# A squared-ReLU MLP on one Trainium2 core: accumulators, unit order and priorities around its first product

## The chip, the core and the metric

The kernel runs on one core of a Trainium2 chip. The metric is the device time of one execution in microseconds (us). In the traces PE is TensorE (matmuls), DVE is VectorE, ACT is ScalarE, POOL is GpSimd and SP issues the DMAs. Each of these engines works through its own list of instructions in order; an instruction that waits holds up all that stand behind it on that engine.

## The reference

One decoder block over 512 tokens of width 1024: two attention mixers, then an MLP of inner width 4096, all in float32.

```python
h = modulate(rmsnorm(x, g_mix), sh_a, sc_a); z = h @ w_in
...  # NSA and MLA attention, gated sum y
x = x + gt_a * (y @ w_out)
h = modulate(rmsnorm(x, g_mlp), sh_m, sc_m)
x = x + gt_m * (square(relu(h @ w_fc1)) @ w_fc2)
return rmsnorm(x, g_final)
```

The change concerns the line with `w_fc1` and `w_fc2` alone.

## The kernel before

**Arithmetic.** Values lie feature by feature on the 128 partitions with the 512 tokens along the row. A float32 operand is split into a rounded part (`hi`, written by ACT) and a rest (`lo`, written by DVE), and each product is three matmuls: hi by hi, hi by lo, lo by hi (`mm3`, L196 to L199). The split of a weight tile starts from its raw load (`w_raw`, four buffers) and stands in `wsplit` (L183 on ACT, L184 on DVE).

**Stages of the MLP.** The inner width is worked off in four quarters (`qq`, L953), which I call q0 to q3. A quarter has eight units of 128 inner features. A unit is a product of 24 matmuls with 512 columns into one accumulator in PSUM (`dense`, lines L197 to L199); in q0 the first four units are computed together in four accumulators. Then `unit_parts` (L908) turns the accumulator into operands of the second product: relu (L911, ACT), squares, differences, and hi and lo parts. Units 0 to 3 give `uh`, `ul` (L923, L924); unit k+4 gives its own `uh`, `ul` (L932, L933) and, together with the stored parts of unit k, the operands called t2, t3 and t4 (L940 to L948).

**Second product.** It takes two output features blocks at a time (`fc2_pair`), by a scheme of seven products instead of eight (Winograd's form of Strassen's algorithm), each of 12 matmuls with 256 columns (L854). Its weights need four sums of raw weight blocks (`wsum`, L825, POOL), each split into `ws_hi` (L811, ACT) and `ws_lo` (L812, DVE). A quarter has four such pairs; q3 has two, and its other four output blocks are done at the end by plain products (L977 on). The seven products accumulate in four half tiles: pa and pb (tag `s`), pc and pd (tag `t`). In the first pair of a quarter (`fresh`) they are interleaved, with a loop that takes the first three of the four inner blocks ahead of the last one (L868). The sums `u` and `e` in `ue` are built outside: copies on ACT (L864, L867), additions on DVE (L873: `e += pc`, L874: `u += pd`), then `v` and the outputs `xr` (L893 to L900). The addition of L873 has to read pc before the last product (a22 by t4) goes on accumulating there.

**What sets the order.** A scheduler lays out each engine's list when the program is built; instructions under `tc.high_priority()` go ahead of others that are ready. Tiles are handed out by tag from a fixed number of buffers: in PSUM two for `acc`, two for `s`, two for `t`, one each for `o` and `m`. The raw weights share four buffers, freed when both splits and the sums have read them.

Of the kernel before, what the change touches and what calls it, by code (L numbers as in the profile page):

```python
# [12 lines left out]
AF = mybir.ActivationFunctionType  # L13
ALU = mybir.AluOpType
PSUM = bass.MemoryType.PSUM

P = 128
S = 512
D = 1024
KT = D // P  # L20
# [18 lines left out]
NPRE = 4  # L39
FAR = 2  # L40
# [6 lines left out]
def block_kernel(ctx: ExitStack, tc: tile.TileContext, d):  # L47
    nc = tc.nc
# [3 lines left out]
    def psum(tag):  # L52
        bufs = PB[tag]
        return ps.tile([P, S], F32, name="ps_" + tag, tag=tag, bufs=bufs)
# [237 lines left out]
    for j in range(4):  # L292
        t = big_n(f"qn{j}")
# [401 lines left out]
    for step in ORDER.split():  # L695
        op, a = step[0], int(step[1:] or 0)
# [35 lines left out]
    for i in range(8):  # L732
        if i < 4:
            t = sb.tile([P, 1280], F32R, name="ohl", tag="p", bufs=NB["p"])[:, 0:1024].rearrange("p (a b) -> p a b", a=2)
# [67 lines left out]
            nc.scalar.activation(xt[n][:, tok], xt[n][:, tok], AF.Copy, scale=cols[:, C_GFIN + n:C_GFIN + n + 1])  # L802

    HS = S // 2
    T0, T1 = HALVES
    ngt = sb.tile([P, KT], F32, name="ngt")
    nc.vector.tensor_scalar(ngt, modb[:, GTM:GTM + KT], -1.0, None, op0=ALU.mult)
# [6 lines left out]
    def pair_weights(src0, src1):  # L814

        raw = [wtile() for _ in range(2)]
        nc.sync.dma_start(raw[1], src1)
        nc.sync.dma_start(raw[0], src0)
        a11, a12 = raw[0][:, 0:S], raw[0][:, S:D]
        a21, a22 = raw[1][:, 0:S], raw[1][:, S:D]  # L820
        sums = []
        for x_, y_ in ((a21, a22), (a11, a21), (0, a11), (2, a12)):
            t = sb.tile([P, S], F32, name="wsum", tag="pT", bufs=NB["pT"])
            with tc.high_priority():
                nc.gpsimd.tensor_tensor(t, sums[x_] if isinstance(x_, int) else x_, y_, op=ALU.add)  # L825
            sums.append(t)
        out = {}

        def part(hi, lo):
            pat = dict(a=4, b=P)  # L830
            return hi.rearrange("p (a b) -> p a b", **pat), lo.rearrange("p (a b) -> p a b", **pat)

        hi = sb.tile([P, D], F32R, name="w_hi", tag="w_hi", bufs=NB["hi"])
        lo = sb.tile([P, D], F32R, name="w_lo", tag="w_lo", bufs=NB["lo"])
        split_part(raw[0], hi, lo)
        out["a11"] = part(hi[:, 0:S], lo[:, 0:S])
        out["a12"] = part(hi[:, S:D], lo[:, S:D])
        for names, ids in ((("s1", "s3"), (0, 1)), (("s2", "s4"), (2, 3))):
            hi = sb.tile([P, 1280], F32R, name="ws_hi", tag="p", bufs=NB["p"])
            lo = sb.tile([P, 1280], F32R, name="ws_lo", tag="p", bufs=NB["p"])  # L840
            for j, (nm_, i) in enumerate(zip(names, ids)):
                c = slice(S * j, S * j + S)
                split_part(sums[i], hi[:, c], lo[:, c])
                out[nm_] = part(hi[:, c], lo[:, c])
        hi = sb.tile([P, D], F32R, name="w_hi", tag="w_hi", bufs=NB["hi"])
        lo = sb.tile([P, D], F32R, name="w_lo", tag="w_lo", bufs=NB["lo"])
        split_part(a22, hi[:, 0:S], lo[:, 0:S])
        out["a22"] = part(hi[:, 0:S], lo[:, 0:S])
        return out

    def product(out, w, x, first, ks=range(4)):
        for k in ks:
            for j, (a_, b_) in enumerate(((0, 0), (0, 1), (1, 0))):
                nc.tensor.matmul(out, w[a_][:, k], x[k][b_], start=(first and k == 0 and j == 0),  # L854
                                 stop=(k == 3 and j == 2), skip_group_check=True)

    def pair_tiles(w, b, sink, fresh):

        pa, pb = psum("s")[:, 0:HS], psum("s")[:, 0:HS]
        pc, pd = psum("t")[:, 0:HS], psum("t")[:, 0:HS]  # L860
        ue = tmp("ue")
        u, e = ue[:, 0:HS], ue[:, HS:S]
        product(pa, w["a11"], b["11"], True)
        nc.scalar.activation(u, pa, AF.Copy)  # L864
        product(pb, w["s1"], b["t1"], True)
        if fresh:
            nc.scalar.activation(e, pb, AF.Copy)  # L867
            for ks in (range(3), range(3, 4)):  # L868
                product(pa, w["a12"], b["21"], False, ks)
                product(pb, w["s4"], b["22"], False, ks)  # L870
                product(pc, w["s3"], b["t3"], True, ks)
                product(pd, w["s2"], b["t2"], True, ks)
            nc.vector.tensor_tensor(e, e, pc, op=ALU.add)  # L873
            nc.vector.tensor_tensor(u, u, pd, op=ALU.add)  # L874
        else:
            product(pc, w["s3"], b["t3"], True)
            nc.scalar.activation(e, pc, AF.Copy)
            nc.vector.tensor_tensor(e, e, pb, op=ALU.add)
            product(pd, w["s2"], b["t2"], True)
            nc.vector.tensor_tensor(u, u, pd, op=ALU.add)  # L880
            product(pa, w["a12"], b["21"], False)
            product(pb, w["s4"], b["22"], False)
        product(pc, w["a22"], b["t4"], False)
        sink(pa, pb, pc, u, e)
# [23 lines left out]
    def unit_parts(n, pa, ub, keep, last):  # L908

        r = tmp("relu")  # L910
        nc.scalar.activation(r, pa, AF.Relu)  # L911
        hh = big_n(f"uh{n}", F32R)
        hl = big_n(f"ul{n}", F32R)
        if n < 4:
            if n < 3:
                raw = small_c(f"ur{n}")
            else:
                raw = sb.tile([P, S], F32, name="ur3", tag="qst", bufs=NB["qst"])
            b12 = keep["b12"][:, n * HS:n * HS + HS]
            nc.scalar.activation(b12, r[:, T1], AF.Square)  # L920
            nc.scalar.activation(raw[:, T0], r[:, T0], AF.Square)
            nc.vector.tensor_tensor(raw[:, T1], raw[:, T0], b12, op=ALU.subtract)
            nc.scalar.activation(hh, raw, AF.Copy)  # L923
            nc.vector.tensor_tensor(hl, raw, f(hh), op=ALU.subtract)  # L924
            ub["11"].append((hh[:, T0], hl[:, T0]))
            ub["t1"].append((hh[:, T1], hl[:, T1]))
            keep["raw"].append(raw)
            keep["b12s"].append(b12)
            return
        k = n - 4  # L930
        nc.scalar.activation(r, r, AF.Square)
        nc.scalar.activation(hh, r, AF.Copy)  # L932
        nc.vector.tensor_tensor(hl, r, f(hh), op=ALU.subtract)  # L933
        ub["21"].append((hh[:, T0], hl[:, T0]))
        ub["22"].append((hh[:, T1], hl[:, T1]))

        raw, b12 = keep["raw"][k], keep["b12s"][k]
        t2, t4 = raw[:, T1], raw[:, T0]
        t3 = tmp("t3")[:, T0] if last else b12
        nc.vector.tensor_tensor(t3, r[:, T1], b12, op=ALU.subtract)  # L940
        nc.vector.scalar_tensor_tensor(t2, t2, -1.0, r[:, T1], op0=ALU.mult, op1=ALU.subtract)
        nc.vector.scalar_tensor_tensor(t4, t2, -1.0, r[:, T0], op0=ALU.mult, op1=ALU.subtract)
        t3p = big_n(f"t3{k}", F32R)
        nc.scalar.activation(t3p[:, T0], t3, AF.Copy)
        nc.vector.tensor_tensor(t3p[:, T1], t3, f(t3p[:, T0]), op=ALU.subtract)
        th_ = sb.tile([P, 2, S], F32R, name="t24", tag="kk", bufs=4)
        nc.scalar.activation(th_[:, 0], raw, AF.Copy)
        nc.vector.tensor_tensor(th_[:, 1], raw, f(th_[:, 0]), op=ALU.subtract)  # L948
        ub["t2"].append((th_[:, 0, T1], th_[:, 1, T1]))
        ub["t4"].append((th_[:, 0, T0], th_[:, 1, T0]))  # L950
        ub["t3"].append((t3p[:, T0], t3p[:, T1]))

    for qq in range(4):  # L953
        ub = {c: [] for c in ("11", "21", "22", "t1", "t2", "t3", "t4")}
        keep = dict(b12=sb.tile([P, D], F32, name="b12", tag="cb"), raw=[], b12s=[])
        pre = {}
        if qq == 0:
            ws = [wsplit(d["w_fc1"][n], (KT, P), n < FAR) for n in range(NPRE)]
            pre = {n: psum(("acc", "acc", "s", "s")[n]) for n in range(NPRE)}
            for tok in HALVES:  # L960
                for k in range(KT):
                    for n in range(NPRE):
                        mm3(pre[n][:, tok], (ws[n][0][:, k], ws[n][1][:, k]),
                            (h2[k][0][:, tok], h2[k][1][:, tok]), k == 0, k == KT - 1)
        for n in range(8):
            if n in pre:
                pa = pre[n]
            else:
                w = wsplit(d["w_fc1"][8 * qq + n], (KT, P))
                pa = psum("acc")  # L970
                dense(pa, w, h2)
            unit_parts(n, pa, ub, keep, qq == 3)
        nf = KT - NH2 if qq == 3 else KT
        for n in range(0, nf, 2):
            fc2_pair(qq, n)
# [138 lines left out]
```

## Time and profile before

| what | value |
|---|---|
| median of 3 runs | 853.53 us (853.52 to 855.48) |
| the profiled execution's own time | 856.97 us |
| its span from first to last instruction | 855.2 us |
| PE busy | 806.6 us, 94% |
| DVE busy | 614.0 us, 72% |
| ACT busy | 394.7 us, 46% |
| POOL busy | 137.6 us, 16% |
| mean granted TensorE clock | 0.981 |

The span leaves out 1.8 us around the program, and the profiled execution is 3.4 us above the median. Times inside the trace are counted from the start of the span. [...] The MLP runs from about 480 us to the end.

### The profile page before, as it was taken

How to read it: one execution, taken by the hardware profiler on the slowest of the kernel's cores; microseconds unless marked ns; L12 is line 12 of the kernel's file. 1: busy time of each engine (PE TensorE's matmuls, PEld its weight loads, DVE VectorE, ACT ScalarE, POOL GpSimd, SP SyncE). 2: the span in 40 equal slices, each digit the busy share in tenths (PEclk: the TensorE clock that was granted, in tenths of full speed). 3: DMA queues.
4: the chain of work that ended last, by engine and by line, in shares of the span. 5: the costliest groups of instructions: out<-in, count | busy, mean ns of one | idle time of the engine just before them, and what ended most of it. 6: DMA issues, size and time to landing. Idle time of an engine off the chain costs nothing.

```text
span 855.2 us, 11874 instructions
## 1 busy us (share of the span) xinstructions
PE 806.6 (94%) x4444; PEld 649.1 (76%) x4444; DVE 614.0 (72%) x1193; ACT 394.7 (46%) x742; POOL 137.6 (16%) x109
## 2 busy tenths in 40 slices
PE   6899999999999999999799989999989998999896
PEld 3687668665586657888679978897789878987795
DVE  6979569878658873568875858866777487757864
ACT  4458436556226443222323556435733464346651
POOL 2400000000001000003300030613242143404100
PEclk8999999999999999999989998999999999999998
DMA  9773342000141204687564121333223322322302
GB/s 337 259 247 111 126 146 73 27 25 30 45 134 64 79 33 160 205 272 217 171 223 152 66 75 50 99 123 99 74 75 122 101 74 74 124 99 77 96 1 99
DMA packets 31003, 99.75 MB, mean 117 GB/s; under 512 B 3521, under 2 KB 5761, under 8 KB 30946
## 3 DMA queue, kind: packets, MB, share of 16 engines
q1 hardware_dynamic: 30880, 98.89, 35.0%
q8 instruction: 35, 0.57, 0.3%
q0 software_dynamic: 64, 0.11, 0.1%
q14 instruction: 22, 0.18, 0.1%
q10 hardware_dynamic: 2, 0.00, 0.0%
HBM read 96.89 MB, written 2.10 MB: 116 GB/s over the span
## 4 chain that ended last, share of the span: by engine, by line
PE 67%; DVE 14%; ACT 6%; POOL 5%; DMA 4%; issue 3%; SPq 0%; POOLq 0%; DVEq 0%; ACTq 0%
PE ps_acc L197 11%; PE ps_acc L198 10%; PE ps_acc L199 10%; PE ps_s L854 7%; PE ps_t L854 6%; POOL wsum L825 4%; PE ps_t L391 3%; PE ps_o L568 3%; DVE junk L107 3%; DVE ws_lo L812 3%; PE ps_s L640 2%; PE ps_o L653 2%; DMA w_raw<-in_w_ada_dram 2%; DMA w_raw<-in_w_fc_dram 2%; POOL yb L758 1%
## 5 line engine op out<-in xcount | busy, mean ns | idle before, releaser
L183 ACT ACTIVATE w_hi<-w_raw 128x1024 fp32r<-128x1024 f32 x76 | 80.2, 1058 | 134.7 <-PE ps_acc L198 96.2
L184 DVE TENSOR_TENSOR w_lo<-w_raw,w_hi 128x1024 fp32r<-128x1024 f32 x76 | 96.7, 1275 | 63.6 <-ACT w_hi L183 63.6
L197 PE MATMUL ps_acc<-h2h,w_hi 128*128 128x512 f32 x224 | 88.9, 397 | 7.7 <-ACT relu L911 7.7
L198 PE MATMUL ps_acc<-h2l,w_hi 128*128 128x512 f32 x224 | 88.4, 395 | 0.0
L199 PE MATMUL ps_acc<-h2h,w_lo 128*128 128x512 f32 x224 | 88.2, 394 | 0.0
L346 ACT ACTIVATE p<-p,nm 128x128 f32<-128x128 f32 (+3 forms) x96 | 53.3, 556 | 58.2 <-DVE nm L344 56.9
L198 PE MATMUL ps_acc<-hl,w_hi 128*128 128x512 f32 x200 | 80.1, 400 | 0.0
L199 PE MATMUL ps_acc<-hh,w_lo 128*128 128x512 f32 x200 | 80.0, 400 | 0.0
L197 PE MATMUL ps_acc<-hh,w_hi 128*128 128x512 f32 x200 | 79.4, 397 | 0.0
L825 POOL TENSOR_TENSOR wsum<-w_raw 128x512 f32<-128x512 f32 x28 | 40.4, 1447 | 176.1 <-DMA w_raw<-in_w_fc_dram 148.7
L379 DVE COPY pT<-ps_t 128x512 f32<-128x512 f32 (+1 forms) x72 | 42.4, 598 | 31.3 <-PE ps_o L568 16.6
L811 ACT ACTIVATE ws_hi<-wsum 128x512 fp32r<-128x512 f32 x56 | 35.4, 631 | 63.8 <-POOL wsum L825 57.5
L825 POOL TENSOR_TENSOR wsum<-wsum,w_raw 128x512 f32<-128x512 f32 x28 | 48.4, 1727 | 85.4 <-DVE ws_lo L812 85.1
L812 DVE TENSOR_TENSOR ws_lo<-wsum,ws_hi 128x512 fp32r<-128x512 f32 x56 | 55.0, 1011 | 7.5 <-PE ps_acc L198 6.3
L197 PEld LDWEIGHTS ps_acc<-h2h,w_hi 128*128 128x128 f32 x224 | 42.7, 191 | 18.2 <-ACT relu L911 9.4
L107 DVE SCALAR_TENSOR_TENSOR junk<-w_raw,cb 128x1024 bf16<-128x1024 f32 x32 | 40.0, 1255 | 15.3 <-DMA w_raw<-in_w_ada_dram 15.1
L199 PEld LDWEIGHTS ps_acc<-h2h,w_lo 128*128 128x128 f32 x224 | 42.8, 191 | 9.1
L198 PEld LDWEIGHTS ps_acc<-h2l,w_hi 128*128 128x128 f32 x224 | 42.8, 191 | 8.7
L198 PEld LDWEIGHTS ps_acc<-hl,w_hi 128*128 128x128 f32 x200 | 37.6, 188 | 10.9 <-issue 4.3
L199 PEld LDWEIGHTS ps_acc<-hh,w_lo 128*128 128x128 f32 x200 | 37.6, 188 | 10.0 <-issue 3.1
L197 PEld LDWEIGHTS ps_acc<-hh,w_hi 128*128 128x128 f32 x200 | 37.6, 188 | 9.9 <-issue 3.0
L854 PE MATMUL ps_t<-t,ws_hi 128*128 128x256 f32 x224 | 41.1, 281 | 0.0
(457 smaller groups left out, 2108.7 us busy)
## 6 DMA issues: line engine op xcount, KB each, us to landing
w_raw<-in_w_fc_dram SPq DMA_DIRECT2D x64, 512.0 KB, 3.3
w_raw<-in_w_ada_dram SPq DMA_DIRECT2D x32, 512.0 KB, 4.2
w_raw<-in_w_z_dram SPq DMA_DIRECT2D x25, 512.0 KB, 3.8
w_ada<-in_w_ada_dram SPq DMA_DIRECT2D x16, 512.0 KB, 6.1
w_raw<-in_w_c_dram SPq DMA_DIRECT2D x8, 512.0 KB, 4.4
w_raw<-in_w_o_dram SPq DMA_DIRECT2D x8, 512.0 KB, 4.2
w_raw<-in_w_out_dram SPq DMA_DIRECT2D x8, 512.0 KB, 3.5
w_raw<-in_w_g_dram SPq DMA_DIRECT2D x8, 448.0 KB, 6.7
```

What stands on the lines that cost most here:

```text
L107: nc.vector.scalar_tensor_tensor(junk, w, 1.0, cb, op0=ALU.mult, op1=ALU.mult, accum_out=mod[:, col:col + 1])
L183: nc.scalar.activation(hi[:, :n], raw[:, :n], AF.Copy)
L184: nc.vector.tensor_tensor(lo[:, :n], raw[:, :n], f(hi[:, :n]), op=ALU.subtract)
L197: nc.tensor.matmul(out, w[0], x[0], start=first, stop=False)
L198: nc.tensor.matmul(out, w[0], x[1], start=False, stop=False)
L199: nc.tensor.matmul(out, w[1], x[0], start=False, stop=last)
L346: nc.scalar.activation(o, o, AF.Exp, bias=nm, scale=-1.0, accum_out=sm)
L379: nc.vector.tensor_copy(dst, src)
L811: nc.scalar.activation(hi, src, AF.Copy)
L812: nc.vector.tensor_tensor(lo, src, f(hi), op=ALU.subtract)
L825: nc.gpsimd.tensor_tensor(t, sums[x_] if isinstance(x_, int) else x_, y_, op=ALU.add)
L854: nc.tensor.matmul(out, w[a_][:, k], x[k][b_], start=(first and k == 0 and j == 0), stop=(k == 3 and j == 2), skip_group_check=True)
```

## The change

It has five parts. The units of a quarter are computed in the order 0 4 1 5 2 6 3 7 (and their weights loaded so). The accumulators of the units rotate over four places, two of tag `acc` and the single buffers of `m` and `o`. The relu gets high priority and the weight sums on POOL lose it. The subtraction that begins t3 goes from DVE to POOL. In the first pair of a quarter pc comes before pb in the loop, pd's whole product follows after the loop, and `e += pc` gets high priority.

```diff
+    UNITS = (0, 4, 1, 5, 2, 6, 3, 7)
@@ pair_weights
-            with tc.high_priority():
-                nc.gpsimd.tensor_tensor(t, sums[x_] if isinstance(x_, int) else x_, y_, op=ALU.add)
+            nc.gpsimd.tensor_tensor(t, sums[x_] if isinstance(x_, int) else x_, y_, op=ALU.add)
@@ pair_tiles, if fresh
             for ks in (range(3), range(3, 4)):
                 product(pa, w["a12"], b["21"], False, ks)
+                product(pc, w["s3"], b["t3"], True, ks)
                 product(pb, w["s4"], b["22"], False, ks)
-                product(pc, w["s3"], b["t3"], True, ks)
-                product(pd, w["s2"], b["t2"], True, ks)
-            nc.vector.tensor_tensor(e, e, pc, op=ALU.add)
+            with tc.high_priority():
+                nc.vector.tensor_tensor(e, e, pc, op=ALU.add)
+            product(pd, w["s2"], b["t2"], True)
             nc.vector.tensor_tensor(u, u, pd, op=ALU.add)
@@ unit_parts
-        nc.scalar.activation(r, pa, AF.Relu)
+        with tc.high_priority():
+            nc.scalar.activation(r, pa, AF.Relu)
...
-        nc.vector.tensor_tensor(t3, r[:, T1], b12, op=ALU.subtract)
+        nc.gpsimd.tensor_tensor(t3, r[:, T1], b12, op=ALU.subtract)
@@ the loop over quarters
-            ws = [wsplit(d["w_fc1"][n], (KT, P), n < FAR) for n in range(NPRE)]
+            ws = [wsplit(d["w_fc1"][UNITS[n]], (KT, P), n < FAR) for n in range(NPRE)]
...
-        for n in range(8):
-            if n in pre:
-                pa = pre[n]
+        for i, n in enumerate(UNITS):
+            if i in pre:
+                pa = pre[i]
             else:
                 w = wsplit(d["w_fc1"][8 * qq + n], (KT, P))
-                pa = psum("acc")
+                pa = psum(("acc", "acc", "m", "o")[i % 4])
                 dense(pa, w, h2)
             unit_parts(n, pa, ub, keep, qq == 3)
```

The lines of the changed kernel stand one or two below those of the kernel before (the relu is L913, `e += pc` still L873, `u += pd` L875).

**First place: ACT in q1, from the weights of the last unit but some on.** Before, the list around the relu of the fourth unit (numbers behind a name tell buffers apart, `b` is the tile b12):

```order
L183 ACTIVATE w_hi<-w_raw 128x1024
L811 ACTIVATE ws_hi<-wsum 128x512 x3
L911 ACTIVATE relu<-ps_acc 128x512
L920 ACTIVATE b_5119<-relu 128x256
L921 ACTIVATE ur_5278<-relu 128x256
L923 ACTIVATE uh_5276<-ur_5278 128x512
L183 ACTIVATE w_hi<-w_raw 128x1024
```

Now, from the relu of the fourth unit in time (unit 5) to the operand of the seventh (unit 3, `uh_5417`):

```order
L913 ACTIVATE relu<-ps_o 128x512
L812 ACTIVATE ws_hi<-wsum 128x512 x3
L933 ACTIVATE relu<-relu 128x512
...
L183 ACTIVATE w_hi<-w_raw 128x1024
L913 ACTIVATE relu<-ps_acc 128x512
...
L913 ACTIVATE relu<-ps_acc 128x512
L812 ACTIVATE ws_hi<-wsum 128x512
L933 ACTIVATE relu<-relu 128x512
L934 ACTIVATE uh_5370<-relu 128x512
...
L925 ACTIVATE uh_5417<-ur_5419 128x512
```

The relu now stands ahead of the splits of the weight sums, and the work behind the relu (squares, `uh`) behind them. The weights of the eighth unit (the last `w_hi` of the first list, the only L183 of the second) stood behind the short parts of unit 3, three operations, and stand behind the parts of unit 5 now: its square, its `uh`, t3 and t24. Unit 3, which was fourth, is seventh, and its `uh` comes behind a `ws_hi` of the second pair and the parts of unit 6.

**Second place: DVE in the first pair of q1.** Before:

```order
L893 SCALAR_TENSOR_TENSOR xr_3166<-ps_s,modb,xr_3166 128x256
L812 TENSOR_TENSOR w_lo<-w_raw,w_hi 128x512
L812 TENSOR_TENSOR ws_lo<-wsum,ws_hi 128x512 x3
L873 TENSOR_TENSOR ue<-ue,ps_t 128x256
L812 TENSOR_TENSOR ws_lo<-wsum,ws_hi 128x512
L874 TENSOR_TENSOR ue<-ue,ps_t 128x256
L897 TENSOR_TENSOR v_5600<-ue,ps_s 128x256
```

Now:

```order
L894 SCALAR_TENSOR_TENSOR xr_3166<-ps_s,modb,xr_3166 128x256
L873 TENSOR_TENSOR ue<-ue,ps_t 128x256
L813 TENSOR_TENSOR ws_lo<-wsum,ws_hi 128x512 x2
L813 TENSOR_TENSOR w_lo<-w_raw,w_hi 128x512
L813 TENSOR_TENSOR ws_lo<-wsum,ws_hi 128x512 x2
L875 TENSOR_TENSOR ue<-ue,ps_t 128x256
L900 TENSOR_TENSOR v_5598<-ue,ps_t 128x256
L813 TENSOR_TENSOR w_lo<-w_raw,w_hi 128x1024
L898 TENSOR_TENSOR v_5600<-ue,ps_s 128x256
```

`e += pc` (L873) moved ahead of all five splits of weights; `u += pd` (L874, now L875) stands behind all five instead of four, and the `v` that frees pb (L897, now L898) behind six, one of them of 1024 columns.

**Third place: POOL in q2.** Now, with the subtraction L942 between the sums:

```order
L942 TENSOR_TENSOR b_6004<-relu,b_6004 128x256
L825 TENSOR_TENSOR wsum<-w_raw 128x512 x2
L825 TENSOR_TENSOR wsum<-wsum,w_raw 128x512 x2
L942 TENSOR_TENSOR b_6004<-relu,b_6004 128x256
L825 TENSOR_TENSOR wsum<-w_raw 128x512 x2
L825 TENSOR_TENSOR wsum<-wsum,w_raw 128x512
L942 TENSOR_TENSOR b_6004<-relu,b_6004 128x256 x2
```

Before, POOL had no L942; the second one now stands behind the four sums of a pair's weights, the last two behind three more.

## Rows read from the trace of the kernel before

**Rows 1.** The page's line on the engines: busy us, share of the span, instructions.

```profile
PE 806.6 (94%) x4444; PEld 649.1 (76%) x4444; DVE 614.0 (72%) x1193; ACT 394.7 (46%) x742; POOL 137.6 (16%) x109
```

**Rows 2.** The stretches of q1 and q2: from and to, then length, busy time of each engine with its instructions, granted clock, share and rate of the DMAs.

```profile
571.00:661.00 90.00, 85.09 (x530) 75.98 (x529) 63.37 (x94) 44.95 (x77) 27.73 (x20) 1.00 0.29 94
661.00:751.00 90.00, 84.98 (x530) 75.84 (x529) 63.30 (x94) 44.79 (x77) 27.76 (x20) 1.00 0.29 94
```

**Rows 3.** PE's waits over the whole span: what waited, for whom; us in total, times, longest.

```profile
PE ps_t L854 <- DVE ue L873: 8.3, 4, 2.1
PE ps_acc L197 <- ACT relu L911: 7.7, 4, 3.3
PE ps_s L854 <- ACT ue L864: 3.2, 3, 1.8
```

**Rows 4.** Timeline of PE: start, duration of one matmul (they overlap, so the step between starts is what counts), operation, and the idle time before it with what ended it. The first matmul of q1 and the first of its second unit; the last wait in q1's units; the first matmul of q1's first pair and its two waits; the first of the fourth pair; the first of q2.

```profile
570.76 0.40 PE L197 MATMUL ps_acc<-h2h,w_hi 128*128 128x512 f32 x1
...
576.24 0.39 PE L197 MATMUL ps_acc<-h2h,w_hi 128*128 128x512 f32 x1
...
599.72 0.50 PE L197 MATMUL ps_acc<-h2h,w_hi 128*128 128x512 f32 x1 [1.57 <-ACT relu L911]
...
616.18 0.28 PE L854 MATMUL ps_s<-uh,w_hi 128*128 128x256 f32 x1
...
619.84 0.39 PE L854 MATMUL ps_s<-uh,w_hi 128*128 128x256 f32 x1 [0.65 <-ACT ue L864]
...
629.25 0.39 PE L854 MATMUL ps_t<-t,w_hi 128*128 128x256 f32 x1 [2.06 <-DVE ue L873]
...
650.69 0.28 PE L854 MATMUL ps_s<-uh,w_hi 128*128 128x256 f32 x1
...
660.63 0.40 PE L197 MATMUL ps_acc<-h2h,w_hi 128*128 128x512 f32 x1
```

**Rows 5.** PE in q0, columns as in rows 4: the wait in the units and the wait in the first pair.

```profile
513.32 0.79 PE L197 MATMUL ps_acc<-h2h,w_hi 128*128 128x512 f32 x1 [3.31 <-ACT relu L911]
...
539.36 0.50 PE L854 MATMUL ps_t<-t,w_hi 128*128 128x256 f32 x2 [2.06 <-DVE ue L873]
```

**Rows 6.** q0 in short stretches, columns as in rows 2.

```profile
510.00:515.00 5.00, 1.69 (x5) 1.40 (x5) 4.86 (x4) 3.55 (x8) 5.00 (x4) 0.77 0.07 29
515.00:520.00 5.00, 5.00 (x14) 3.85 (x14) 4.96 (x9) 4.94 (x10) 0.23 (x1) 0.55 0.07 18
...
535.00:541.00 6.00, 3.94 (x30) 3.73 (x29) 5.93 (x8) 2.27 (x4) 4.12 (x3) 0.92 0.52 163
541.00:546.00 5.00, 5.00 (x35) 5.00 (x35) 3.40 (x6) 2.41 (x5) 2.93 (x3) 0.76 0.04 16
```

**Rows 7.** PE in q3, columns as in rows 4: the three waits before the tail.

```profile
779.37 0.50 PE L197 MATMUL ps_acc<-h2h,w_hi 128*128 128x512 f32 x1 [1.32 <-ACT relu L911]
...
800.74 0.39 PE L854 MATMUL ps_s<-uh,w_hi 128*128 128x256 f32 x1 [1.79 <-ACT ue L864]
...
810.05 0.51 PE L854 MATMUL ps_t<-t,w_hi 128*128 128x256 f32 x2 [2.06 <-DVE ue L873]
```

**Rows 8.** Timeline of ACT in q1: start, duration, operation, idle time before and what ended it.

```profile
598.55 0.63 ACT L811 ACTIVATE ws_hi<-wsum 128x512 fp32r<-128x512 f32 x1 [1.05 <-POOL wsum L825]
599.09 0.58 ACT L911 ACTIVATE relu<-ps_acc 128x512 f32<-128x512 f32 x1
...
601.66 1.05 ACT L183 ACTIVATE w_hi<-w_raw 128x1024 fp32r<-128x1024 f32 x1
...
608.92 0.64 ACT L811 ACTIVATE ws_hi<-wsum 128x512 fp32r<-128x512 f32 x1 [1.20 <-POOL wsum L825]
...
613.77 0.58 ACT L911 ACTIVATE relu<-ps_acc 128x512 f32<-128x512 f32 x1
```

**Rows 9.** Timeline of DVE in q1, columns as in rows 8: the split of a unit's weights; the subtraction L940; the run of splits ahead of L873.

```profile
593.62 2.06 DVE L184 TENSOR_TENSOR w_lo<-w_raw,w_hi 128x1024 fp32r<-128x1024 f32 x1 [1.12 <-ACT w_hi L183]
...
601.79 0.69 DVE L924 TENSOR_TENSOR ul<-ur,uh 128x512 fp32r<-128x512 f32 x1 [0.70 <-ACT uh L923]
602.74 1.23 DVE L184 TENSOR_TENSOR w_lo<-w_raw,w_hi 128x1024 fp32r<-128x1024 f32 x1 [0.26 <-ACT w_hi L183]
...
604.40 0.42 DVE L940 TENSOR_TENSOR b<-relu,b 128x256 f32<-128x256 f32 x1 [0.44 <-ACT relu L931]
...
610.74 0.67 DVE L940 TENSOR_TENSOR b<-relu,b 128x256 f32<-128x256 f32 x1 [0.77 <-ACT relu L931]
...
625.30 0.69 DVE L812 TENSOR_TENSOR w_lo<-w_raw,w_hi 128x512 fp32r<-128x512 f32 x1
625.91 2.96 DVE L812 TENSOR_TENSOR ws_lo<-wsum,ws_hi 128x512 fp32r<-128x512 f32 x3
628.79 0.41 DVE L873 TENSOR_TENSOR ue<-ue,ps_t 128x256 f32<-128x256 f32 x1
```

**Rows 10.** Timeline of POOL in q1, columns as in rows 8.

```profile
598.94 1.27 POOL L825 TENSOR_TENSOR wsum<-w_raw 128x512 f32<-128x512 f32 x1 [0.42 <-DMA w_raw<-in_w_fc_dram]
...
608.85 2.27 POOL L825 TENSOR_TENSOR wsum<-wsum,w_raw 128x512 f32<-128x512 f32 x1
...
633.08 0.73 POOL L895 TENSOR_TENSOR v<-ue 128x256 f32<-128x256 f32 x1
```

## The prediction

> **What bounds the kernel now.** I read the page's engines first, then PE's waits, then PE's timeline in the MLP, and only then the engines it waits for. PE is busy for 94% of the span and DVE for 72% [rows 1], so a gain can only come from PE's waits or from its time at the lower clock. The reader should see in the list of waits that three lines of the MLP stand together: PE waits 7.7 us for relu, 8.3 us for `e += pc` on DVE and 3.2 us for the copy `ue` [rows 3], 19.2 us in all. q1 and q2 are alike to 0.1 us of busy PE and run at a granted clock of 1.00 [rows 2], so one of them stands for both.
>
> How long would a quarter be without waits? In q1 the units take 616.18 - 570.76 = 45.42 us with one wait of 1.57 us, so 43.85 us for eight, or 5.48 each, which is also the step from the first unit to the second [rows 4]. The fourth pair, which shows no wait, takes 660.63 - 650.69 = 9.94 us [rows 4]. Eight units and four pairs make 83.6 us; the quarter takes 660.63 - 570.76 = 89.87. **6.3 us** of q1 is waiting and restarting.
>
> In q0 the wait for relu is 3.31 us, and that for `e += pc` 2.06 us [rows 5]. Behind each stands a stretch below full clock. Behind the first it is 0.55 for 5 us (2.25 us lost), and about 0.5 from 513.3 to 515 (0.85 us); behind the second 0.76 for 5 us (1.2 us) and 0.92 over 6 us (0.5 us) [rows 6]. [...] In q1, a wait of 2.06 us shows no such loss [rows 2, 4]. q0 thus has 3.31 + 3.1 + 2.06 + 1.7 = **10.2 us** to give. q3 has 1.32 + 1.79 + 2.06 = **5.2 us** [rows 7]. With q1 and q2 the total is 10.2 + 6.3 + 6.3 + 5.2 = **28.0 us**, all that these edits could remove.
>
> **What each part does to it.** *Four accumulators and the relu ahead.* Before, a unit needs the accumulator of the unit two before it. ACT has three `ws_hi` ahead of that relu, and the last of them waits 1.05 us for POOL [rows 8]. Now a unit needs the accumulator of four units before, and its relu stands ahead of the sums. The relu waits go, in every quarter.
>
> *The order of units.* This is where I think time comes back. Unit 3 is now seventh. The first product of the first pair needs its `ul` at the eleventh of its matmuls. I replay q1 with durations of the trace, counted from its first matmul. The last `ws_hi` ahead of unit 5's parts starts at 598.55 - 570.76 = 27.8 [rows 8]. Unit 5's parts take as long as from `ws_hi` to the next relu behind such parts now: 613.77 - 608.92 = 4.85 [rows 8], less the moved relu (0.53) and the 0.5 of a short `w_hi`, so 3.8 us. I add 1.2 for the third part below, where the subtraction stands behind a sum of 1.27 us on POOL [rows 10]. The weights of the eighth unit are then split from 32.8 on, where they were at 601.66 - 570.76 = 30.9 [rows 8]. Their `w_hi` takes 1.05 and their `w_lo` 1.23 [rows 8, 9]: end at 35.1. That frees the raw buffer for the second pair's weights; from such an end to the sum on POOL 3.26 us pass (593.62 + 2.06 to 598.94) [rows 9, 10], and the sum takes 1.27. So the `ws_hi` ahead of unit 6's parts starts near 39.8. Behind it come again 4.3 us up to unit 3's relu, and from relu to the end of `ul` 602.48 - 599.09 = 3.4 us [rows 8, 9]: **47.5**. PE wants it at 43.85 + 1.2 = 45.0. So a new wait of about **2.6 us** in place of the relu's. In q0 the same replay gives 3.5 us. Its bounds: none if ACT gets through with POOL on time; 4.5 us if the sum takes 2.27 as the second row of POOL shows [rows 10].
>
> *t3's subtraction on POOL.* It costs DVE 0.42 alone and 0.67 while POOL works [rows 9]; on POOL I take 0.73, what the addition of the same size takes [rows 10]. All 16 would cost 16 x 0.31 = 5 us if each were on the path; only the ones ahead of t24 in the chain above are, and I have counted them there. That POOL and DVE hinder each other is in the rows: L940 takes 0.42 or 0.67, a split of 1024 columns 1.23 or 2.06 [rows 9]. [...]
>
> *The first pair.* Before, `e += pc` stands behind a split of 0.69 and three of 2.96 together [rows 9], and PE waits 2.06 us for it. Now it is ahead of them, and pd's product of 12 matmuls (1.42 us, a seventh of 9.94) covers it. That wait goes in all four quarters. What is late next: `u += pd`, behind four `ws_lo` (4 x 0.99) and a `w_lo` (0.69), 4.6 us after L873 [rows 9]. PE gets there after pd, a22 and the next pair's first product, 3 x 1.42 = 4.3 us after pc, and needs `v` behind it (0.41) as well. I put the wait at 1.4 us from my replay, and 0.7 more for the `v` that frees pb, which now has a split of 1.23 us ahead of it. So **2.1 us** per quarter; bounds 0, if POOL leaves DVE alone (a split then takes 0.69), and 4.4, if the splits run as slow as the 2.06 row. The wait for the copy `ue` goes, since PE arrives later.
>
> *Sums lose priority on POOL.* POOL does little else [rows 1]; I cost it at nothing beyond the place of L942.
>
> **Sum.** Out: 28.0. In: 4 x 2.1 for the additions on DVE, 2.6 each in q1, q2 and q3, 3.5 in q0, 1.7 for a stretch at 1.2 GHz behind q0's new wait, since it is as long as the 3.31 us one that brought a stretch there [rows 5, 6]. 8.4 + 7.8 + 3.5 + 1.7 = 21.4. Net **6.6 us faster**: q0 2.9, q1 and q2 1.6 each, q3 0.5. The profiled execution of 856.97 would become 850.4; from the median of 853.53 it is **846.9 us**.
>
> **The rivals.** *A, the units are on time.* If ACT reaches unit 3's parts before PE needs them, 3 x 2.6 + 3.5 + 1.7 = 13.0 us of the new waits fall away: 846.9 - 13 = **834**. For it speaks that unit 3's accumulator is complete at 7 x 5.48 = 38.4, and the bare chain of 3.4 us would end before 45.0; against it that ACT is in order and the `ws_hi` in front hangs on a load. The point is whether that `ws_hi` starts before 37.3.
>
> *B, slower: the new wait brings the lower clock in every quarter.* At q0's 3.31 us the clock fell, at 2.06 in q1 it did not. If the sum on POOL takes 2.27 and the wait grows by 1.5 us, to 4.1, q1 to q3 cross that mark: each loses 1.5 + 1.7 and a further 1 on DVE, which POOL then holds up; 3 x 4.2 + 2.5 in q0 = 15 us against 6.6 gained: **862**, and with half of it 855. It decides from about 1.6 us more per quarter than I take. Against it: three of the four waits of 2 us had no such cost. [...]
>
> *C, no change.* The waits only change their names: the additions on DVE reach their bound of 4.4 us, 4 x 2.3 = 9.2 more than I take, or 2 to 3 more with the clock kept: **851 to 856**. Or the rotation does nothing because `m` and `o` are still held; nothing in a quarter uses these tags, so this is small.
>
> **How the numbers follow.** Forecast (gain of 3 to 11 us) 0.54; A and what lies between 0.17; C 0.17; B 0.12. About 0.3%, 2.6 us, is what a measurement of this kernel can tell from no change. All of A and the forecast is faster, and a little of C: faster 0.72, same 0.15, slower 0.13. The range leaves out most of A below and B's worst above: **836 to 856**; the forecast's own is 842.5 to 850.5.
>
> **What would show it.** In the profile after: no PE wait for relu and none for L873; a new PE wait of 2 to 4 us for `ul` (L926) or `uh` near the third matmul group of each quarter's first pair; waits for `v` or `u` (L875, L898, L900) of about 2 us in the second pair; a quarter of about 88.3 us instead of 89.9; L942 on POOL near 0.73 us. The forecast is wrong if the first pair starts without the wait for unit 3 (A), or if the granted clock of q1 or q2 falls under 0.98 (B).

## The result: 0.5% faster, with the forecast's mechanism and without its gain in q0

Over ten runs each the change takes 852.13 us (849.86 to 855.32) and the kernel before 856.5 us (853.52 to 861.32). The ratio is **0.9946, 95% interval 0.9926 to 0.9967**: 2.8 to 6.3 us faster, 4.6 in the middle. The forecast said 6.6; its 846.9 us counted from 853.53, the median of the first three runs, and from 856.5 the same gain leads to 849.9. The profiled execution took 852.93 us with a span of 851.2; against the 855.2 of before it gained 4.0.

The waits of PE over the whole span of the changed kernel (what waited, for whom; us, times, longest), those in the MLP:

```profile
PE ps_s L854 <- ACT uh L925: 6.8, 5, 2.7
PE ps_t L854 <- DVE ue L875: 4.9, 4, 1.5
...
PE ps_s L854 <- DVE v L898: 2.9, 7, 0.6
...
PE ps_s L854 <- DVE ul L926: 1.4, 4, 0.4
PE ps_s L854 <- ACT ue L864: 1.1, 1, 1.1
```

All three waits of [rows 3] are gone or small: none for relu, none for L873, 1.1 us for the copy. In their place stand the two that were forecast: 8.2 us for unit 3's `uh` and `ul`, 7.8 us for the additions L875 and L898 on DVE. Of 19.2 us there are 17.1 left.

PE's timeline of the changed kernel (start, duration of one matmul, idle time before it and what ended it): q0's first pair from its start, then the first matmul of q1, q1's first pair, and the first matmul of q2. These answer to [rows 4, 5].

```profile
520.48 0.28 PE L854 MATMUL ps_s<-uh,w_hi 128*128 128x256 f32 x1
...
522.13 0.39 PE L854 MATMUL ps_s<-uh,w_hi 128*128 128x256 f32 x1 [0.79 <-ACT uh L925]
522.89 0.39 PE L854 MATMUL ps_s<-ul,w_hi 128*128 128x256 f32 x1 [0.37 <-DVE ul L926]
...
526.10 0.58 PE L854 MATMUL ps_s<-uh,w_hi 128*128 128x256 f32 x1 [2.70 <-ACT uh L925]
526.83 0.58 PE L854 MATMUL ps_s<-ul,w_hi 128*128 128x256 f32 x1
527.21 0.41 PE L854 MATMUL ps_s<-uh,w_lo 128*128 128x256 f32 x1
...
570.59 0.40 PE L197 MATMUL ps_acc<-h2h,w_hi 128*128 128x512 f32 x1
...
614.15 0.28 PE L854 MATMUL ps_s<-uh,w_hi 128*128 128x256 f32 x1
616.46 0.38 PE L854 MATMUL ps_s<-uh,w_hi 128*128 128x256 f32 x1 [1.08 <-ACT uh L925]
617.19 0.39 PE L854 MATMUL ps_s<-ul,w_hi 128*128 128x256 f32 x1 [0.34 <-DVE ul L926]
617.41 0.28 PE L854 MATMUL ps_s<-uh,w_lo 128*128 128x256 f32 x1
...
629.13 0.51 PE L854 MATMUL ps_t<-t,ws_hi 128*128 128x256 f32 x2 [1.51 <-DVE ue L875]
631.36 0.38 PE L854 MATMUL ps_s<-uh,ws_hi 128*128 128x256 f32 x1 [0.58 <-DVE v L898]
...
658.89 0.40 PE L197 MATMUL ps_acc<-h2h,w_hi 128*128 128x512 f32 x1
```

q1 lasts 658.89 - 570.59 = 88.30 us, where it was 89.87 [rows 4]: 1.57 gained. q0's first pair would have its twelfth matmul 1.3 us after its start (eleven steps of 0.12), near 521.8; it starts at 527.21, so PE lost 5.4 us there, with three idle times of 3.86 us together, and the steps behind 526.10 are already slow (0.38 us from 526.83 to 527.21). In q1 the twelfth matmul, due at 614.15 + 1.3, starts at 617.41: 1.95 us lost. Two stretches of q0 in the changed kernel (length, busy time of each engine, granted clock, DMA share and rate) answer to [rows 6]:

```profile
522.00:527.00 5.00, 1.64 (x5) 0.94 (x6) 4.63 (x9) 4.73 (x11) 0.29 (x1) 0.78 0.35 121
527.00:535.00 8.00, 8.00 (x51) 8.00 (x52) 4.54 (x8) 3.94 (x9) 0.97 (x1) 0.71 0.01 2
```

The clock is 0.71 over 8 us: behind the wait PE again has a stretch below full clock, which costs 0.29 x 8 = 2.3 us. There is a second such stretch, in q3, behind the wait for unit 3, which is there of nearly the same length as in q1:

```profile
793.07 0.39 PE L854 MATMUL ps_s<-uh,w_hi 128*128 128x256 f32 x1 [1.13 <-ACT uh L925]
793.80 0.39 PE L854 MATMUL ps_s<-ul,w_hi 128*128 128x256 f32 x1 [0.34 <-DVE ul L926]
```

```profile
794.00:798.00 4.00, 4.00 (x22) 4.00 (x22) 3.74 (x7) 3.49 (x8) 0.97 (x1) 0.57 0.00 1
```

It costs 0.43 x 4 = 1.7 us; before, q3 ran at 1.00 up to the tail, from 751 to 820 us. In q1 and q2 of the changed kernel the clock stays at 1.00. The lengths of the parts of the MLP by the first matmul of each, before and after, in us:

| kernel (label of the run) | q0 | q1 | q2 | q3 | tail | MLP |
|---|---|---|---|---|---|---|
| before | 86.03 | 89.87 | 90.02 | 69.44 | 35.11 | 370.5 |
| the change | 86.13 | 88.30 | 88.27 | 69.41 | 34.59 | 366.7 |
| units 0 to 7 (e1_order) | 85.52 | 88.34 | 88.34 | 69.07 | 34.58 | 365.9 |
| t3 on DVE (e2_dve) | 85.10 | 89.37 | 87.30 | 68.65 | 34.88 | 365.3 |
| two accumulators (e3_twoacc) | 86.71 | 88.26 | 88.24 | 69.28 | 34.59 | 367.1 |
| first pair as before (e4_pair) | 87.55 | 89.57 | 89.61 | 68.69 | 34.84 | 370.3 |
| splits of sums later (f1_split) | 86.25 | 86.48 | 86.59 | 66.35 | 34.60 | 360.3 |
| sums on DVE in q0 alone (h1_q0) | 77.45 | 88.02 | 88.16 | 68.70 | 34.60 | 356.9 |
| sums on DVE (f2_wsumdve) | 77.47 | 83.34 | 83.34 | 66.47 | 34.59 | 345.2 |
| sums and t3 on DVE (f5_wsumdve_t3dve) | 76.71 | 83.34 | 83.34 | 66.67 | 34.58 | 344.6 |
| before, with sums on DVE (g1_before_sums) | 83.49 | 89.42 | 89.47 | 65.59 | 34.59 | 362.6 |
| all on DVE, idle work on POOL (g2_load) | 88.69 | 92.92 | 92.48 | 72.12 | 34.59 | 380.8 |

What lies ahead of the MLP differs by some 4 us between profiles of programs that are alike there, so I compare the MLP's parts in profiles, and whole times by ratios to runs of the kernel before on the same chip.

### The profile page after: what moved, and what is told of

It reads as the page before. It is cut to its first block, busy times and chain, and to the rows that moved or that the text cites. A ratio compares the mean times of both kernels' runs of the same rounds, so it can differ in the third digit from the quotient of the medians.

```text
span 851.2 us, 11895 instructions
## 1 busy us (share of the span) xinstructions
PE 805.5 (95%) x4444; PEld 650.0 (76%) x4444; DVE 611.8 (72%) x1177; ACT 393.0 (46%) x742; POOL 151.2 (18%) x125
## 4 chain that ended last, share of the span: by engine, by line
PE 61%; DVE 15%; DMA 7%; issue 6%; ACT 5%; POOL 5%; SPq 0%; POOLq 0%; DVEq 0%; ACTq 0%
PE ps_acc L197 8%; PE ps_acc L198 8%; PE ps_acc L199 8%; PE ps_s L854 7%; PE ps_t L854 4%; DMA w_raw<-in_w_ada_dram 4%; PE ps_t L391 3%; PE ps_o L568 3%; DVE junk L107 3%; POOL wsum L825 3%; DMA w_raw<-in_w_fc_dram 3%; PE ps_s L640 2%; DVE ws_lo L813 2%; DVE w_lo L184 2%; PE ps_o L653 2%
## 5 line engine op out<-in xcount | busy, mean ns | idle before, releaser
L183 ACT ACTIVATE w_hi<-w_raw 128x1024 fp32r<-128x1024 f32 x76 | 80.3, 1058 | 134.9 <-PE ps_acc L198 86.5
L812 ACT ACTIVATE ws_hi<-wsum 128x512 fp32r<-128x512 f32 x56 | 35.2, 631 | 65.6 <-POOL wsum L825 55.7
L813 DVE TENSOR_TENSOR ws_lo<-wsum,ws_hi 128x512 fp32r<-128x512 f32 x56 | 46.8, 867 | 7.2 <-PE ps_acc L198 6.3
L197 PE MATMUL ps_acc<-h2h,w_hi 128*128 128x512 f32 x112 | 43.6, 390 | 0.0
L199 PE MATMUL ps_acc<-h2h,w_lo 128*128 128x512 f32 x112 | 43.6, 389 | 0.0
L198 PE MATMUL ps_acc<-h2l,w_hi 128*128 128x512 f32 x112 | 43.6, 389 | 0.0
L758 POOL TENSOR_TENSOR yb<-ya,yb 128x512 f32<-128x512 f32 x8 | 17.5, 2184 | 135.1 <-DVE yb L757 125.0
L854 PE MATMUL ps_s<-uh,w_hi 128*128 128x256 f32 x112 | 33.1, 296 | 7.9 <-ACT uh L925 6.8
L391 PEld LDWEIGHTS ps_t<-ident,p 128*128 128x128 f32 x240 | 27.7, 141 | 16.4 <-issue 6.3
```

What stands on the lines that cost most here:

```text
L183: nc.scalar.activation(hi[:, :n], raw[:, :n], AF.Copy)
L197: nc.tensor.matmul(out, w[0], x[0], start=first, stop=False)
L198: nc.tensor.matmul(out, w[0], x[1], start=False, stop=False)
L199: nc.tensor.matmul(out, w[1], x[0], start=False, stop=last)
L391: nc.tensor.transpose(pp[:, off:off + P], aps[i][:, kb * P:(kb + 1) * P], ident)
L813: nc.vector.tensor_tensor(lo, src, f(hi), op=ALU.subtract)
```

## The experiments

**First the parts of the change, undone one at a time.** The order of units:

```diff
-    UNITS = (0, 4, 1, 5, 2, 6, 3, 7)
+    UNITS = (0, 1, 2, 3, 4, 5, 6, 7)
```

> The change with the units of a quarter in the order 0 to 7 as before; its other parts stay. Theory: unit 3 as the seventh unit makes the new wait at the first pair (in the profile after, 5.1 us of waiting in q0 with some 1.8 us of lower clock behind it, and 1.8 us in each of q1 to q3). Without the order it goes: 5.1 + 1.8 + 3 x 1.8 = 12 us, so the span falls from 851 to about 839, no PE wait for L925 or L926, q0 about 79 us long, q1 and q2 86.5. Rival 1: the chain is late because POOL and DVE hold each other up (t3's subtraction on POOL), whatever the order; then the first pair waits for unit 7 or for an operand t2 to t4 instead, and the span stays within 3 us of 851. Rival 2: the time comes back as a wait for the additions on DVE (L875, L898), since PE arrives earlier there: a gain of 6 us instead of 12.

The ratio to before is 0.9945 (0.9926 to 0.9965), the same as the change's. My theory fell, and of rival 1 the span came true (849.1). The wait for unit 3 went, and one of the same length came a product later, for the copy `ue` that stands on ACT behind the parts of unit 7. PE in this run, in q0's first pair:

```profile
527.37 0.58 PE L854 MATMUL ps_s<-uh,w_hi 128*128 128x256 f32 x1 [5.11 <-ACT ue L864]
```

So the order decides where PE meets the late engines, not how late they are.

t3's subtraction:

```diff
-        nc.gpsimd.tensor_tensor(t3, r[:, T1], b12, op=ALU.subtract)
+        nc.vector.tensor_tensor(t3, r[:, T1], b12, op=ALU.subtract)
```

> The change with t3's subtraction back on DVE; its other parts stay. Theory (the order makes the wait): the wait for unit 3 stays, shorter by what the subtraction and the blocking cost in the chain, 0.3 to 1 us per quarter; span 848 to 851. Rival 1 (the blocking of POOL and DVE makes the wait): the wait for L925 and L926 nearly goes, the span falls by 8 us or more, to 843 or less.

Ratio 0.9937 (0.9916 to 0.9958). The waits for `uh` fell from 6.8 to 4.1 us, in q0 they stayed, with the longest still 2.7. The part alone is worth 1.4 us in the MLP's profile, within what two measurements differ by. In its q1 PE waits 1.8 us for a `v`, and the clock is 0.61 from 632 to 636 behind it; q2, without that, takes 87.30.

The accumulators:

```diff
-                pa = psum(("acc", "acc", "m", "o")[i % 4])
+                pa = psum("acc")
```

> The change with only the two accumulators of tag acc for the later units; its other parts stay (order 0 4 1 5 2 6 3 7, relu first). Theory: the relu ahead of the weight sums is not enough, PE needs the accumulator of the unit two before, and in q0 ACT reaches the relu of the seventh unit some 7 us after its product ended; so relu waits come back in place of part of the wait for unit 3: a wait of 2 to 5 us in q0, under 1 us in q1 and q2 (the relu stands ahead of the sums there), the wait at the first pair shorter by as much. Span 850 to 854. Rival: the priority of the relu alone removes the waits and the four accumulators do nothing: the span as in the change, 851, and no wait for relu at all.

Ratio 0.9950 (0.9932 to 0.9968). The relu waits came back with 3.9 us in all, and the wait at the first pair shrank by as much (43.2 instead of 44.7 us for q1's pairs, 45.05 instead of 43.56 for its units). The theory's trade holds; its 2 to 5 us in q0 were under 1. Here four accumulators by themselves buy nothing that can be measured.

The first pair of a quarter, in the order of before and with `e += pc` without priority:

> The change with the first pair of a quarter in the order of before and e += pc without priority; its other parts stay. Theory: the wait of 2.1 us for L873 comes back in each quarter, and the waits for L875 (1.2 to 1.5 us) and most of that for L898 go: the net of this part is about zero, +-0.5 us per quarter, so the span is 849 to 853. Rival: the reordering of the pair is what gives the 1.6 us in q1 and q2: the span rises by 5 us or more, to 856 or more.

Ratio 1.0030 (1.0012 to 1.0048), against the change's 0.9946. The rival was right: without this part the change gains nothing. The profile shows half of the loss, 370.3 us of MLP against 366.7; its execution, 854.59 us, is among the fastest of its runs, whose median is 858.4. The wait for L873 is back with 8.2 us. By the list of waits alone that is no more than the 7.8 us for L875 and L898 that it replaces; but in q1 waits of 0.6 for the copy `e` (L867) and of 0.6 for L878 and `v` stand beside it, 3.2 us together where the change has 2.4, and in q2 the clock is 0.58 for 4 us behind it.

The third part, the priorities of the relu and of the weight sums, was not undone on its own.

**Then the lateness itself: who waits for POOL's sums, and who is held up by them.** The splits of the sums without priority:

```diff
-                split_part(sums[i], hi[:, c], lo[:, c])
+                split_part(sums[i], hi[:, c], lo[:, c], False)   # not in high_priority
```

> The change with the splits of the four weight sums (ws_hi on ACT, ws_lo on DVE) without high priority, so that ACT's list has most of the units' parts ahead of them. The run with the old unit order moved the wait of q0 from the operand uh to the copy ue (5.1 us) without shortening it. Theory A: ACT reaches the late units late because ws_hi in front waits for the sums on POOL (1.69 + 0.80 + 1.45 + 0.75 = 4.7 us in q0, 0.35 + 1.59 + 1.07 + 2.07 = 5.1 us in q1 in the profile after). Then q0's first-pair wait of 5.1 us falls under 2 us and the lower clock behind it (some 1.8 us) goes, q1 to q3 lose 1 to 1.8 us each: span 843 or less. Theory B: the slow operations on DVE beside POOL make it (1.2 to 2.3 us instead of 0.4 to 1.2): the wait at the first pair keeps over 3 us in q0, span 849 to 853. Rival C: the splits come too late for the second pair and a new wait for ws_lo takes the place: span over 851.

Ratio 0.9881 (0.9858 to 0.9905). Theory A holds for q1 to q3, which gained 1.7 to 3.1 us each, the waits for L875 gone among them. It does not hold for q0: PE's longest wait there is 5.0 us still, and q0 takes 86.25. ACT, whose list has the splits of the sums later, now waits in q0's units for DVE and for t3's subtraction (L946), which stands on POOL behind a sum that lasts 4.95 us, where the mean of a sum is 1.4 to 1.7 in the change. What makes it so long was not shown; in the change t3's subtraction took 0.74 us on POOL at 503.08, with DVE idle, and 0.98 at 611.57, begun 0.04 us after an operation of DVE's. In f1_split:

```profile
510.78 0.63 ACT L953 ACTIVATE t<-ur 128x512 fp32r<-128x512 f32 x1 [3.74 <-DVE ur L948]
514.91 4.95 POOL L829 TENSOR_TENSOR wsum<-w_raw 128x512 f32<-128x512 f32 x1 [4.45 <-DVE ws_lo L813]
520.58 0.42 ACT L950 ACTIVATE t<-b 128x256 fp32r<-128x256 f32 x1 [2.65 <-POOL b L946]
```

The sums on DVE:

```diff
-            nc.gpsimd.tensor_tensor(t, sums[x_] if isinstance(x_, int) else x_, y_, op=ALU.add)
+            nc.vector.tensor_tensor(t, sums[x_] if isinstance(x_, int) else x_, y_, op=ALU.add)
```

> The change with the four weight sums of a pair on DVE instead of POOL; t3's subtraction stays on POOL. DVE gets 16 more operations of about 0.69 us per quarter (11 us) and loses what POOL's sums cost it. Theory B (DVE and POOL hold each other up): the splits of 512 columns fall from a mean of 0.87 to 0.65 us, those of 1024 to 1.23, no operation of DVE's over 1.3 us in q0's units; the wait at q0's first pair falls from 5.1 to under 2.5 us: span 843 to 847. Theory A (ACT stands behind the sums): a sum now takes 0.69 instead of 1.3 to 2.3 us, so ACT waits less too, and the gain is as large; what tells them apart is ACT's idle time ahead of ws_hi beside DVE's durations. Rival: DVE becomes the bound (it was 72% busy), the additions behind its splits come later, and the span is 853 or more.

Ratio **0.9695 (0.9671 to 0.9719)**, a median of 829.04 us and a span of 827.3. The gain was larger than either theory gave: q1 and q2 take 83.34 us, which is what their products take without any wait (PE is busy for 80.00 of the 80 us from 560 to 640, and again from 640 to 720). What happened on DVE shows in q0's units. The changed kernel, DVE (start, duration, operation):

```profile
504.76 1.78 DVE L935 TENSOR_TENSOR ul<-relu,uh 128x512 fp32r<-128x512 f32 x1
506.47 1.51 DVE L943 SCALAR_TENSOR_TENSOR ur<-ur,relu 128x256 f32<-128x256 f32 x1
507.90 2.31 DVE L184 TENSOR_TENSOR w_lo<-w_raw,w_hi 128x1024 fp32r<-128x1024 f32 x1
510.14 2.98 DVE L813 TENSOR_TENSOR ws_lo<-wsum,ws_hi 128x512 fp32r<-128x512 f32 x3
...
515.19 1.78 DVE L950 TENSOR_TENSOR t<-ur,t 128x512 fp32r<-128x512 f32 x1
516.89 1.52 DVE L944 SCALAR_TENSOR_TENSOR ur<-ur,relu 128x256 f32<-128x256 f32 x1
```

and POOL beside it:

```profile
504.56 1.44 POOL L825 TENSOR_TENSOR wsum<-w_raw 128x512 f32<-128x512 f32 x1 [0.74 <-DMA w_raw<-in_w_fc_dram]
505.95 3.18 POOL L825 TENSOR_TENSOR wsum<-wsum,w_raw 128x512 f32<-128x512 f32 x2
```

The same DVE operations with the sums on DVE:

```profile
502.83 0.69 DVE L935 TENSOR_TENSOR ul<-relu,uh 128x512 fp32r<-128x512 f32 x1
503.43 0.42 DVE L943 SCALAR_TENSOR_TENSOR ur<-ur,relu 128x256 f32<-128x256 f32 x1
503.77 1.22 DVE L184 TENSOR_TENSOR w_lo<-w_raw,w_hi 128x1024 fp32r<-128x1024 f32 x1
```

1.78 against 0.69, 1.51 against 0.42, 2.31 against 1.22: each of these, beside a sum, takes 1.1 us more, and as each starts the sum on POOL has 1.2 us left. And the sums that DVE takes over cost it next to nothing on balance. q1 with the sums on POOL, in the changed kernel (engines in the order PE, PEld, DVE, ACT, POOL):

```profile
571.00:659.00 88.00, 84.18 (x528) 75.70 (x528) 62.38 (x89) 44.14 (x77) 31.45 (x24) 1.00 0.28 96
```

and q1 with sums and t3's subtraction on DVE (f5_wsumdve_t3dve):

```profile
557.00:641.00 84.00, 84.00 (x535) 76.45 (x534) 63.88 (x110) 44.52 (x77) 3.57 (x4) 1.00 0.30 101
```

DVE is busy for 63.9 us instead of 62.4, with 21 operations more in the stretch.

> The change with both the weight sums and t3's subtraction on DVE, so that POOL has only the small v of each pair. Against the run with the sums alone on DVE this shows what the subtraction on POOL is worth without the sums there: theory, within 1 us of that run (16 x 0.42 us on DVE against 16 x 0.73 on POOL, mostly off the path). If DVE is the bound, it is slower by 2 us or more.

Ratio 0.9684 (0.9659 to 0.9710), against 0.9695: no difference that can be told, as the theory had it.

That leaves two causes mixed, since with the sums on DVE nobody waits for POOL either. So POOL got work that nobody reads, with all that others need on DVE:

```diff
+            for c in HALVES:
+                nc.gpsimd.tensor_tensor(idle, (a11 if isinstance(x_, int) else x_)[:, c], y_[:, c], op=ALU.add)
```

> The change with sums, t3's subtraction and v all on DVE, and with POOL doing additions that nothing reads: eight of 128x256 per pair on the same raw weights, into a tile of its own (0.73 us each, 5.9 us per pair, about what the four sums took). No instruction on ACT, DVE or PE waits for POOL's results; only the raw weight buffers wait for its reads. Theory B (the blocking itself is the price): DVE's splits and sums beside POOL take 1.2 to 2 us again, the waits at q0's first pair come back, and the span rises from 825 to 838 or more. Theory A (ACT and DVE waited for POOL's results): the span stays within 4 us of 825.

Ratio 1.0117 (1.0095 to 1.0140): slower than before by 10 us. Against f5_wsumdve_t3dve, which has no such work (and `v` on POOL), the MLP of the profile is 36 us longer. A stretch of the length of q1 (the last 10 us of q0, and q1 without its last 10), DVE in q0's units, and PE's wait in the first pairs of the four quarters:

```profile
560.00:653.00 93.00, 87.31 (x531) 78.92 (x530) 78.05 (x114) 44.37 (x78) 32.11 (x32) 0.96 0.28 94
```

```profile
506.44 1.23 DVE L929 TENSOR_TENSOR ul<-ur,uh 128x512 fp32r<-128x512 f32 x1
507.59 1.23 DVE L953 TENSOR_TENSOR t<-ur,t 128x512 fp32r<-128x512 f32 x1
508.74 1.23 DVE L938 TENSOR_TENSOR ul<-relu,uh 128x512 fp32r<-128x512 f32 x1
```

```profile
PE ps_s L857 <- ACT uh L928: 14.3, 4, 3.8
```

POOL is busy for 32.1 us, as with the sums (31.5), and DVE for 78.1 instead of 63.9, of which the four `v` are some 1.7. Behind the wait the clock fell in each quarter (in q0 to 0.50 from 525 to 529). Theory B came true: with nobody waiting for POOL's additions, DVE's operations last longer (the `ul` of L938 1.01 us on average, where the same operation took 0.69 in f5_wsumdve_t3dve), and what stands behind them is late. The raw buffers, which wait for POOL's reads too, are not the reason: DVE waits 3.4 us in all for loads of raw weights here, and 5.7 in f5_wsumdve_t3dve.

Then the term that failed:

```diff
-        w = pair_weights(d["w_fc2"][qq, n], d["w_fc2"][qq, n + 1])
+        w = pair_weights(d["w_fc2"][qq, n], d["w_fc2"][qq, n + 1], nc.vector if qq == 0 else nc.gpsimd)
```

> The change with the weight sums on DVE in q0 alone; q1 to q3 keep theirs on POOL. The forecast gave q0 a gain of 2.9 us and it had none (86.1 us in both profiles). Theory: in q0's units DVE's operations run blocked beside POOL's sums, at two to four times what the forecast priced them, and that is the whole of the step's error and more. Then q0 takes 77 to 78.5 us as with all sums on DVE, with no PE wait for L925 over 0.5 us in it and the clock at 1.00, while q1 and q2 keep 88.3 and q3 69.4: span about 842.5. Rival: q0's units are late because four of them end at once and ACT has their parts in a row; then q0 still takes over 82 us.

Ratio 0.9842 (0.9824 to 0.9860), the MLP 356.9 us. q0 takes 77.45 us instead of 86.13, and q1 and q2 keep their length. One wait of 0.9 us is left in q0, for the copy `ue`, and the clock holds; the rival, over 82 us, falls. Its units and first pairs in this run:

```profile
482.00:518.50 36.50, 36.48 (x222) 32.76 (x222) 25.36 (x48) 22.87 (x46) 4.42 (x3) 1.00 0.15 45
518.50:560.00 41.50, 40.63 (x340) 40.33 (x339) 37.90 (x67) 20.09 (x36) 5.01 (x5) 1.00 0.35 114
```

ACT's waits for POOL's sums (4.7 us in q0) went with the sums, so this run alone does not split them from DVE's slow operations. f1_split, where ACT no longer stood behind the sums and q0 kept its length, and g2_load, where nobody waits for POOL and the wait is there, speak for DVE.

**What else is worth having.** The one edit in the kernel before:

> The kernel before with one edit: the four weight sums of a pair on DVE instead of POOL (still in high priority). Nothing of the change is in it. Theory: DVE and POOL holding each other up is what made ACT and DVE late in the kernel before too, so most of the 28 us of q0 to q3 go: PE's waits for relu and for L873 fall from 16 us together to under 6, span 830 to 838. Rival: the five parts of the change are needed as well (two accumulators alone make PE wait for each relu, and e += pc stands behind the splits): span 842 or more.

Ratio 0.9902 (0.9885 to 0.9919): the rival's number (a span of 844.8) by one of its two reasons. The waits for relu are gone, with two accumulators and the relu without priority, but PE waits more for L873, since the sums, which have priority here, stand ahead of it on DVE now as well. Behind that wait the clock falls in q0 to q2, to 0.50 from 534 to 538 in q0. Its wait:

```profile
PE ps_t L854 <- DVE ue L873: 13.6, 4, 4.0
```

So the two belong together: the change alone 0.9946, the sums on DVE alone 0.9902, both 0.9695. Which of the change's parts makes the difference was not run; the one long wait that is left here is the one that the new first pair removes, and in the change the sums have no priority.

`u += pd` in high priority too:

> The change with u += pd (L875) in high priority as well as e += pc. Theory: PE's waits for it (4.9 us, four times 1.2) and for the v behind it shrink, at most to half, since L875 then stands behind three instead of five splits: 2 to 4 us less, span 847 to 849. Rival: the splits of the sums come later by as much, and PE waits for ws_lo or for v in the second pair instead: span 850 to 852.

Ratio 0.9979 (0.9960 to 0.9998). The rival was right: the wait for L875 went, but PE waits 7.4 us for the `v` behind it (2.9 in the change) and 2.2 us for `ws_hi`.

Two variants of the best version:

> The change with sums and t3's subtraction on DVE, and the units in the order 0 to 7. With the blocking gone the order should no longer decide: within 2 us of 825.3 in span. If it is more than 2 us slower, the order 0 4 1 5 2 6 3 7 spreads the parts of a unit better (three short parts, then four long ones); if faster, unit 3 as seventh still costs.

Ratio 0.9699 (0.9677 to 0.9722) against 0.9684: the order makes no difference that can be told. q0 to q2 take 76.75, 83.34 and 83.34; q3 takes 68.07 instead of 66.67, with the clock at 0.76 from 791 to 795. The span, 829.4, is 4 us longer where 2 were allowed, but 2.9 of it lies ahead of the MLP.

> The change with sums and t3's subtraction on DVE, and the copy u (L864) in high priority. In the run without it PE waits 2.7 us in q3's second pair, where L864 stands on ACT behind the squares and scalings of the outputs (L130, L907) and the splits of the last weights. Theory: that wait goes and the span falls by 2 to 3 us, to 822 to 823.5. Rival: the work that L864 passes comes later by as much and the tail waits for it: the same 825.

Ratio **0.9671 (0.9649 to 0.9693)**, a median of 827.76 us. In q3 the wait of 2.7 us shrank to 0.6, another of 0.75 came for the copy `e` (L879), and q3 went from 66.67 to 65.63. Whole times don't tell it from 0.9684. This and f5 are the best of what ran: 3.2 and 3.3% under before, 2.6 and 2.8% under the change.

## Why the prediction was right in kind and wrong in size

**The bound, and what goes.** Right. The waits for relu and for L873 went, and PE's waits still set the time. Of the 6.6 us, q0 to q3 gained 3.25 in the profile; of the 3.35 that are missing, 3.0 are q0's.

**q1 and q2.** 1.6 us forecast, 1.57 and 1.75 measured, in part by luck. Against the 83.34 us without waits, q1 loses 5.0 us where 4.7 were forecast: 1.95 for unit 3's operands where the term was 2.6, and the other 3.0 where the additions on DVE had 2.1. The two errors are of opposite sign.

**q0: the step that failed.** The sum gave q0 a gain of 2.9 us and it had -0.1. By the forecast's own base, 86.03 - 10.2 = 75.8 us, the new losses are 10.3 us instead of 7.3. The new wait was sized as 3.5 us ("in q0 the same replay gives 3.5 us"), the clock behind it as 1.7 and the additions as 2.1; PE lost 5.4, 2.3 and 2.6. No run shows the 1.2 GHz of the term for the clock: the profile gives a granted clock as a share, 0.55 over 5 us in q0 before and 0.71 over 8 us in the change. The replay, whose working for q0 the prediction does not give, took DVE's durations from q1, 0.4 to 1.2 us with one sum in the chain. In q0 four units end at once, and their parts stand on DVE just while POOL works through the sums of the first pair and half of the second's: the operations that met one took up to 1.1 us more, some 7 us in all between 504 and 519. h1_q0 shows it: without POOL's sums in q0 that quarter is 8.7 us shorter, with the same units and the same order.

**q3.** 0.5 forecast, 0.03 found. Two terms stood at nothing: the wait for the copy, which was to go "since PE arrives later" and is 1.1 us still, and the clock, which cost 1.7 us behind a wait like those of q1 and q2. Unit 3's term (2.0 lost for 2.6) and that of the additions (idle 0.40 and 0.24 for 2.1) were too large and hid part of it.

**t3's subtraction on POOL.** Priced as a term in the chain and otherwise at nothing; it takes 0.91 us on POOL on average instead of my 0.73. Undone it moves the time by no more than a measurement can tell.

**DVE beside POOL.** I read from the rows that the two hinder each other, and used it for one subtraction. In the change an operation of DVE's in q0 took 1.1 us more beside a sum, in g2_load 0.5 more beside an idle addition, and the trace of before held it as well: L812 took 2.96 us for three where 0.69 was the time of one [rows 9]. What I missed is that it concerned the 56 sums that the change leaves on POOL. The term "all that these edits could remove" of 28.0 us was near the total: with sums and subtraction on DVE, the MLP lost 25.9 of it, 25.3 of them in q0 to q3.

**The rivals.** A (834) did not come with the change; its condition, ACT and DVE on time, is what f2_wsumdve made true. B's lower clock came in q0, where the forecast had it, and in q3, where it had not; q1 and q2 kept 1.00. The "mark" between 2.06 and 3.31 us is not borne out: waits of 1.13 and 0.34 us stand ahead of the stretch in q3, and 1.08 and 0.34 us in q1 had none behind them. C's range, 851 to 856, holds the measured 852.13. Its mechanism holds in part: PE waits 17.1 us where it waited 19.2, most of it under other names; but the additions cost 3 us in q1, not 4.4.

## What to carry to other kernels

When an engine is late, look first at whether its instructions last longer than the same ones do elsewhere in the trace, before reordering what waits for them: here moving the units or adding accumulators only moved the wait (ratios of 0.9945 and 0.9950 without the one or the other, 0.9946 with both). Compare VectorE's busy time with the work on GpSimd and with it on VectorE: here the sums and t3's subtraction on GpSimd saved it next to nothing, 62.4 against 63.9 us in q1. And price a replayed chain with durations from its own stage, with what runs beside it there.

## What the hardware showed that I had not expected

Sixteen sums per quarter, moved to DVE with t3's subtraction, left DVE's busy time nearly as it was, 62.4 against 63.9 us in q1. Additions on POOL that no instruction reads made the MLP 36 us longer (380.8 against 344.6), more than the sums themselves had cost (366.7 against 345.2), though part of the 36 is time at a lower clock (a mean of 0.975 over the span, against 0.99 in f5_wsumdve_t3dve). And the length of a wait did not by itself tell whether the clock falls: q3's wait of 2.7 us for the copy had none behind it in f5_wsumdve_t3dve, and one of 2.6 us at the same place had 0.82 and 0.76 over 8 us in g3_order.
